# Projections: a quad's two first differences behind the weight split, and the fifth quad's sums in the second pair of units

## The chip, the core and the metric

The kernel runs on one core of a Trainium2 chip. TensorE (PE) multiplies, VectorE (DVE), ScalarE (ACT) and GpSimd (POOL) work elementwise, and SyncE (SP) issues most of the transfers. The metric is the device time of one launch in microseconds: the median of three runs, and beside it the span of one profiled execution, from its first to its last instruction.

## The reference

Two layers on a sequence of 256 rows, 2048 wide, with 32 heads of 128, all in float32. Cut to what matters here:

```
h = rms_norm(x, a_norm);  q, k, v, g = split(h @ a_w_in, 4)          # 2048 -> 4 x 4096
o = chunked attention with a relative-position bias
x = x + (o * silu(g)) @ a_w_out                                      # 4096 -> 2048
h_kv = rms_norm(x, kv_norm);  k, v = split(h_kv @ kv_w, 2)           # 2048 -> 2 x 4096
h = rms_norm(x, b_norm);  q, g = split(h @ b_w_in, 2)
o = forgetting attention (causal, decayed by cumulated log gates)
x = x + (o * silu(g)) @ b_w_out                                      # 4096 -> 2048
out = rms_norm(x, final_norm)
```

The change is in the two output projections, `@ a_w_out` (called ao) and `@ b_w_out` (called bo), each 256 x 4096 times 4096 x 2048.

## The kernel before

**Units and blocks.** The 2048 output columns of a projection are four units of 512 columns (ao0 to ao3). A unit sums over 16 blocks of 256 rows of the weight. A block is one transfer of 512 KB into a `raw` buffer (L207, issued by SP; six buffers, `RAW`). Float32 precision comes from splitting every operand in a rounded part and its rest: ACT copies raw to `hi` (L248), DVE subtracts `lo = raw - hi` (L249), and PE multiplies x.hi by w.hi, x.hi by w.lo and x.lo by w.hi (L185). There are four `hi` and four `lo` buffers (`SPLIT`), so the splits run four steps ahead of PE and then wait for PE to free a buffer. A plain block is 12 matmuls: two inner halves, two row tiles, three products.

**Quads.** For some blocks a 2 x 2 product of half blocks is made with seven products instead of eight (`class Quad`). A quad takes block b of two neighbouring units at once, `one` and `two` (two raw buffers), and is four steps for the feeder: i0 splits `one`, i1 splits two differences `t`, i2 splits half of `two`, i3 splits `one` again, after it was overwritten with two more differences. The first differences are `t0 = two0 - one0` (L289) and `t1 = two1 - two0` (L290); the later ones are L298 and L299, which overwrite `one`. Their ACT halves are L295, their DVE halves L296. On PE a quad is 21 matmuls (L528 to L530) and needs four combinations of the activations for its block, the *sums*: five small DVE operations (L380 to L386), an ACT copy (L387) and a DVE rest (L388), made by `Quads.sum_up` one quad after the other when the generator `ao_quads.open` is advanced.

**Order of the work.** `Quads.order` puts the quads between the plain blocks, three plain blocks from one quad to the next. The first pair of units (ao0, ao1) has 13 plain blocks, quad 0, three plain blocks, quad 1, three, quad 2, and the last seven; that is 29 steps. The second pair (ao2, ao3) has four plain blocks and five quads with three blocks between, then six. bo has quads only in its second pair, placed likewise. `project` walks these steps, and after each one lets side work advance by a list of step counts: for `ao_quads.open` the list was `[3, 1, 1, 2, 2]`, so the sums of quad blocks 0 to 4 are made after steps 3, 4, 5, 7 and 9. Block 4 is used by the second pair alone, since the first has three quads.

**What orders the engines.** Each engine works through its queue in order. The order in it is set when the program is built, by a scheduler which places an instruction as soon as what it depends on allows, by its own estimate. Two devices hold an instruction back. `feed.behind(dst, n)` (L265) makes ACT write one column of `dst` from a finished `hi` tile, so that whoever writes `dst` later stands behind that split; it was used for t0's half of `t`. `tc.issue_after(ins)` holds what is issued under it until behind the instruction `ins` in the order; `feed.by_dve` is the last L249 or L296 given out, `feed.by_act` the last L248 or L295. `t1` writes the other half of `t` and was held back by neither.

Of the kernel before, what the change touches and what calls it, by code (L numbers as in the profile page):

```python
# [2 lines left out]

# [49 lines left out]
QUADS = 5  # L53
# [13 lines left out]
def r32(ap):  # L67
    return ap.bitcast(F32)
# [8 lines left out]
def trunk(ctx, tc, x, x_t, gains, a_w_in, a_rel, a_w_out, kv_w, f_w, f_b, b_w_in, b_w_out, final_norm, out):  # L77
    nc = tc.nc
    pe, act, dve, pool, sp = nc.tensor, nc.scalar, nc.vector, nc.gpsimd, nc.sync
# [66 lines left out]
    def finish(side):  # L146
        advance(side, 99)
# [130 lines left out]
    class Quad:  # L278
# [4 lines left out]
        def split(self, i):  # L283

            one, two = self.raw
            t = self.all.t[:, 0]
            if not i:
                feed.behind(t[:, :, 0, :1], -1)
                dve.tensor_sub(t[:, :, 0], two[:, :, 0], one[:, :, 0])  # L289
                dve.tensor_sub(t[:, :, 1], two[:, :, 1], two[:, :, 0])  # L290
            src = [one, t, two[:, :, 1:], one][i]
            n = src.shape[2]
            hi = stream.tile([P, IL, KB, HN], F32R, name=f"quad_hi{i}", tag="hi", bufs=SPLIT)
            lo = stream.tile([P, IL, KB, HN], F32R, name=f"quad_lo{i}", tag="lo", bufs=SPLIT)
            feed.by_act = act.activation(hi[:, :, :n], src, AF.Copy)  # L295
            feed.by_dve = dve.tensor_sub(lo[:, :, :n], src, r32(hi[:, :, :n]))  # L296
            if not i:
                dve.tensor_sub(one[:, :, 0], two[:, :, 1], t[:, :, 0])  # L298
                dve.tensor_sub(one[:, :, 1], one[:, :, 1], one[:, :, 0])  # L299
            return hi, lo  # L300
# [89 lines left out]
    def spec(name, w, nk, late=0, kept=0, g0=None, quads=0):  # L390


        return dict(name=name, w=w, nk=nk, late=late, kept=kept, g0=g0, plain=nk // KB - quads)
# [8 lines left out]
    woven = [(qkvg[u], b) for u, b in WOVEN]  # L402
    todo = woven + [i for i in whole(qkvg[1]) if i not in woven]

    a_quads = Quads("a", None)
    a_pairs = [Quad(a_quads, qkvg[2 * g:2 * g + 2], KD // KB - 1, True, True) for g in range(1, NG)]
    for quad in a_pairs:
        first, second = (whole(sp_) for sp_ in quad.specs)
        todo += first[:QUAD_STEP] + [(None, quad)] + first[QUAD_STEP:] + second
    ao = [spec(f"ao{u}", a_w_out[u], KI) for u in range(4)]  # L410
    ao_quads, bo_quads = Quads("ao", a_w_out), Quads("bo", b_w_out)
    ao_order = ao_quads.order(ao[0], ao[1], 3, 13) + ao_quads.order(ao[2], ao[3], QUADS, 4)
    todo += ao_order
    for g in range(NG):
# [2 lines left out]
    bo = [spec(f"bo{u}", b_w_out[u], KI, LATE if u == 3 else 0, KEPT if u == 3 else 0) for u in range(4)]  # L417
# [6 lines left out]
    feed = Feed(todo)  # L424
# [36 lines left out]
    def project(lhs, specs, order, begun, closed, sides):  # L461


        units = {}

        def get(u):
            if u not in units:
                units[u] = Unit(lhs, specs[u])
            return units[u]

        for sp_, b in order:
            if sp_:
                us = [int(sp_["name"][-1])]
                get(us[0]).step(b)
            else:
                us = [int(u["name"][-1]) for u in b.specs]
                b.step(lhs, *(get(u) for u in us))
            for u in us:
                begun(u, units[u].left)
            for side, steps in sides:  # L480
                if steps:
                    steps[0] -= 1
                    while steps and steps[0] <= 0:
                        next(side, None)
                        steps.pop(0)
            for u in us:
                if not units[u].left:
                    more = closed(u, units[u].acc)
                    if more:
                        sides.append(more)  # L490
        for side, _ in sides:
            finish(side)
# [39 lines left out]
    def attention(g, biases, qk, vg, half, ocat, queues=(pool,) * NQ, line=(None, None), home=None):  # L532
# [50 lines left out]
        gT = z[:, :, HG * NB:].rearrange("p i (t h) u -> p h t i u", t=NT)  # L583
        yield
        ph, pl = split([pT[:, i, :NT] for i in range(HG)], "wide", line[1])
        yield
        op = bank("op").rearrange("p (i s) -> p i s", i=HG)
# [101 lines left out]
    oA = Stat("oA", KI)  # L689

    def side_a(g, accs):
        tb = att.tile([P, HG, S], F32, name="tb", tag="tb")
        for lo_, hi_, c0 in ((0, CHUNK, CHUNK), (CHUNK, P, 0)):
            sp.dma_start(out=tb[lo_:hi_, :, c0:], in_=bass.AP(
                tensor=a_rel.tensor, offset=a_rel.offset + g * HG * NREL + REL + 1 - P + lo_ + c0,
                ap=[[1, hi_ - lo_], [NREL, HG], [1, S - c0]]))

        def biases():
            pool.memset(tb[:CHUNK, :, :CHUNK], NEG)
            return tb[:, :, ::-1], tb[:, :, P - 1::-1]  # L700

        qk = rows(UN, "qk")
        if g:
            for t in range(NT):
                dve.scalar_tensor_tensor(qk[:, t], accs["qk"][t], rsA[:, t:t + 1], a_quads.comb[:, t],
                                         op0=OP.mult, op1=OP.add)
        else:
            evac_scaled(accs["qk"], 0, UN, rsA, qk)
        yield

        def vg():
            return accs["v"], accs["g"]

        yield from attention(g, biases, qk, vg, halfA, oA, (pool, pool, pool, act), (2, 2), home)
# [31 lines left out]
    rs, prev = [], None  # L746
    for g in range(NG):
# [15 lines left out]
        old, prev = prev, side_a(g, accs)  # L763
# [55 lines left out]
                           accum_out=ssq1[:, t, u:u + 1])  # L819
        return more and (more, [8, 7, 1, 1, 1] if u % 2 else [11, 1, 1, 1])  # L820

    project(oA, ao, ao_order, ao_begun, ao_closed, [(prev, [1, 0, 2, 6, 2, 1]), (ao_quads.open(oA, QUADS), [3, 1, 1, 2, 2])])
    tot1 = const.tile([P, NT], F32, name="tot1")
    dve.tensor_reduce(tot1, ssq1, axis=AX.X, op=OP.add)
    rsB, halfB = rstd_of(tot1, "b")
# [73 lines left out]
    def side_b(g, accs):  # L899
        cb = att.tile([P, HG, S], F32, name="cb", tag="tb")  # L900
        sp.dma_start(out=cb, in_=bass.AP(tensor=cumd.tensor, offset=cumd.offset + g * HG * S,
                                           ap=[[0, P], [S, HG], [1, S]]))

        def biases():
            d0 = att.tile([P, HG, P], F32, name="d0")
            for i in range(HG):
                h = g * HG + i
                act.activation(d0[:, i], cb[:, i, :P], AF.Identity, bias=cum[:, 0, h:h + 1], scale=-1.0)
                act.activation(cb[:, i], cb[:, i], AF.Identity, bias=cum[:, 1, h:h + 1], scale=-1.0)
            for ap in (cb[:, :, P:], d0):  # L910
                pool.affine_select(out=ap, in_=ap, compare_op=OP.is_ge, fill=NEG, base=0,
                                   pattern=[[0, HG], [-1, P]], channel_multiplier=1)
            return cb, d0

        qk, gs = accs["q"]
        kv = accs["kv"]
        evac_scaled(kv, 0, GC, rsB, qk[:, :, GC:])
        rest_of = attention(g, biases, qk, lambda: (v, gs), halfB, oB, line=(1, 2), home=home)
        next(rest_of)
        yield  # L920
        v = v_split(kv, GC, rsB)
        yield
        yield from rest_of
# [8 lines left out]
    for g in range(NG):  # L932
# [3 lines left out]
        old, prev = prev, side_b(g, accs)  # L936
# [101 lines left out]
```

## Time and profile before

| | before |
|---|---|
| median of 3 runs | 1744.66 us (1743.78 to 1745.17) |
| the profiled execution | 1746.91 us, of which the span is 1745.2 us |
| granted TensorE clock, mean over the span | 0.998 |
| busy share of the span: PE, DVE, ACT, POOL | 99%, 79%, 65%, 30% |
| matmuls of the ao projection in the span | 697 to 868 us |
| matmuls of the bo projection in the span | 1569 to 1736 us |

A row of the timeline gives start and duration in us, the engine, the line, the operation, the tiles (out<-in), and in brackets the idle time of the engine before it and what ended that. A row of a wait list gives the total in us, how often, and the longest.

### The profile page before, as it was taken

The numbers are of one execution on the slowest core, as the hardware profiler recorded it, in microseconds if no ns is written. First come the engines' busy times: TensorE is split into PE (matmuls) and PEld (weight loads), VectorE is DVE, ScalarE is ACT, GpSimd is POOL, SyncE is SP. The second block draws the span as 40 slices with busy tenths as digits, with TensorE's granted clock in tenths as the row PEclk, the third lists the DMA queues.
The fourth block names the chain that finished last, engine by engine and source line by source line (L and its number), as shares of the span: only waits on it lengthen the run. The fifth ranks groups of instructions, "written<-read, shape, count | busy, mean of one in ns | idle before, by whom it ended". The sixth has DMA issues, their size and how long they took to land.

```text
span 1745.2 us, 25902 instructions
## 1 busy us (share of the span) xinstructions
PE 1725.5 (99%) x8303; PEld 1513.7 (87%) x8303; DVE 1375.6 (79%) x2066; ACT 1140.9 (65%) x2164; POOL 517.0 (30%) x1071
## 2 busy tenths in 40 slices
PE   9999999999999999999999999999999999999997
PEld 7888888888888888888888888888888888888886
DVE  7888888888888888888966777777777777776877
ACT  6666666666666666655657777777777777765554
POOL 1332333333333333112104333333333333333000
PEclk9999999999999999999999999999999999999999
DMA  8777777767777777666767777777777777777654
GB/s 294 247 230 225 235 229 229 232 227 227 225 228 229 231 227 226 196 235 238 245 214 231 227 227 226 227 226 225 226 228 223 227 225 227 250 224 233 225 194 145
DMA packets 143657, 396.38 MB, mean 227 GB/s; under 512 B 31104, under 2 KB 38560, under 8 KB 143392
## 3 DMA queue, kind: packets, MB, share of 16 engines
q1 hardware_dynamic: 107472, 354.25, 63.3%
q0 software_dynamic: 32256, 37.29, 6.6%
q10 hardware_dynamic: 3792, 3.17, 0.6%
q8 instruction: 66, 1.08, 0.3%
q14 instruction: 71, 0.58, 0.1%
HBM read 351.05 MB, written 4.23 MB: 204 GB/s over the span
## 4 chain that ended last, share of the span: by engine, by line
PE 91%; DVE 4%; DMA 3%; ACT 1%; issue 1%; SPq 0%; ACTq 0%; DVEq 0%
PE bkv_acc L185 19%; PE bqg_acc L185 19%; PE aqk_acc L185 16%; PE avg_acc L185 16%; PE bo_acc L185 8%; PE ao_acc L185 3%; DMA ao_raw<-in_a_w_out 2%; DVE ao_lo L249 1%; PE p L530 1%; PE p L529 1%; PE p L528 1%; DVE quad_lo L296 1%; PE s0p L552 1%; PE op L592 1%; PE s1p L530 0%
## 5 line engine op out<-in xcount | busy, mean ns | idle before, releaser
L502 POOL DMA_DIRECT2D sums<-first x448 | 219.9, 498 | 324.6 <-DVE wide L521 147.6
L502 POOL DMA_DIRECT2D sgZ<-sgY x512 | 250.7, 497 | 177.2 <-DVE sgY L499 96.5
L244 DVE SCALAR_TENSOR_TENSOR bqg_lo<-bqg_raw,gain,bqg_hi 128x512 fp32r<-128x512 f32 x256 | 182.8, 750 | 87.4 <-ACT bqg_hi L243 87.4
L243 ACT ACTIVATE bqg_hi<-bqg_raw,gain 128x512 fp32r<-128x512 f32 x256 | 170.9, 714 | 109.1 <-PE bqg_acc L185 51.3
L244 DVE SCALAR_TENSOR_TENSOR bkv_lo<-bkv_raw,gain,bkv_hi 128x512 fp32r<-128x512 f32 x256 | 180.1, 748 | 40.7 <-ACT bkv_hi L243 39.2
L185 PE MATMUL bqg_acc<-bqg_hi,x1Th 128*128 128x512 f32 x512 | 191.4, 384 | 0.0
L185 PE MATMUL bkv_acc<-bkv_hi,x1Th 128*128 128x512 f32 x512 | 189.0, 379 | 0.0
L185 PE MATMUL bkv_acc<-bkv_lo,x1Th 128*128 128x512 f32 x512 | 188.8, 379 | 0.0
L185 PE MATMUL bqg_acc<-bqg_lo,x1Th 128*128 128x512 f32 x512 | 188.8, 379 | 0.0
L185 PE MATMUL bkv_acc<-bkv_hi,x1Tl 128*128 128x512 f32 x512 | 188.8, 379 | 0.0
L185 PE MATMUL bqg_acc<-bqg_hi,x1Tl 128*128 128x512 f32 x512 | 188.8, 379 | 0.0
L243 ACT ACTIVATE bkv_hi<-bkv_raw,gain 128x512 fp32r<-128x512 f32 x256 | 167.5, 712 | 25.9 <-PE bqg_acc L185 20.0
L185 PE MATMUL aqk_acc<-aqk_hi,xTh 128*128 128x512 f32 x452 | 167.6, 382 | 1.4 <-ACT aqk_hi L248 1.4
L185 PE MATMUL avg_acc<-avg_hi,xTh 128*128 128x512 f32 x452 | 167.5, 382 | 0.2 <-ACT avg_hi L248 0.2
L185 PE MATMUL aqk_acc<-aqk_lo,xTh 128*128 128x512 f32 x452 | 166.3, 379 | 1.0 <-DVE aqk_lo L249 1.0
L185 PE MATMUL aqk_acc<-aqk_hi,xTl 128*128 128x512 f32 x452 | 166.1, 379 | 0.0
L185 PE MATMUL avg_acc<-avg_hi,xTl 128*128 128x512 f32 x452 | 166.1, 379 | 0.0
L185 PE MATMUL avg_acc<-avg_lo,xTh 128*128 128x512 f32 x452 | 166.1, 379 | 0.0
L248 ACT ACTIVATE avg_hi<-avg_raw 128x1024 fp32r<-128x1024 f32 x112 | 116.1, 1050 | 75.9 <-PE avg_acc L185 50.3
L249 DVE TENSOR_TENSOR avg_lo<-avg_raw,avg_hi 128x1024 fp32r<-128x1024 f32 x112 | 136.4, 1219 | 31.4 <-ACT avg_hi L248 31.4
L249 DVE TENSOR_TENSOR aqk_lo<-aqk_raw,aqk_hi 128x1024 fp32r<-128x1024 f32 x110 | 134.0, 1222 | 25.4 <-ACT aqk_hi L248 20.3
L248 ACT ACTIVATE aqk_hi<-aqk_raw 128x1024 fp32r<-128x1024 f32 x110 | 115.6, 1051 | 41.7 <-PE avg_acc L185 28.1
(348 smaller groups left out, 3927.5 us busy)
## 6 DMA issues: line engine op xcount, KB each, us to landing
bqg_raw<-in_b_w_in SPq DMA_DIRECT2D x128, 512.0 KB, 4.3
bkv_raw<-in_kv_w SPq DMA_DIRECT2D x128, 512.0 KB, 4.1
avg_raw<-in_a_w_in SPq DMA_DIRECT2D x127, 512.0 KB, 4.7
aqk_raw<-in_a_w_in SPq DMA_DIRECT2D x125, 512.0 KB, 4.6
ao_raw<-in_a_w_out SPq DMA_DIRECT2D x64, 512.0 KB, 4.4
bo_raw<-in_b_w_out SPq DMA_DIRECT2D x64, 512.0 KB, 4.2
sgZ<-sgY POOLq DMA_DIRECT2D x512, 40.0 KB, 4.0
sums<-first POOLq DMA_DIRECT2D x448, 32.0 KB, 3.7
```

The lines of the kernel that those rows point to most:

```text
L185: pe.matmul(acc[t], x[:, t * P:(t + 1) * P], w, start=t not in begun, stop=last and i == 2)
L243: act.activation(hi[:, :, j], raw[:, :, j], AF.Copy, scale=gk)
L244: dve.scalar_tensor_tensor(lo[:, :, j], raw[:, :, j], gk, r32(hi[:, :, j]), op0=OP.mult, op1=OP.subtract)
L248: self.by_act = act.activation(hi[:, :, j], raw[:, :, j], AF.Copy)
L249: self.by_dve = dve.tensor_sub(lo[:, :, j], raw[:, :, j], r32(hi[:, :, j]))
L296: feed.by_dve = dve.tensor_sub(lo[:, :, :n], src, r32(hi[:, :, :n]))
L502: queues[j].dma_start(out=r32(z)[j * SQ:(j + 1) * SQ, i], in_=y[i * SQ:(i + 1) * SQ, j])
L528: pe.matmul(out_, a[0], b[0], start=start, stop=False)
L529: pe.matmul(out_, a[0], b[1], start=False, stop=False)
L530: pe.matmul(out_, a[1], b[0], start=False, stop=stop)
L552: pe.matmul(s0p[:, i], q0[:, i], qkT[:, HG + i, 0], start=True, stop=True)
L592: pe.matmul(op[:, i, 1::NT], v1[:, i * DH:(i + 1) * DH], pT[:, i, NT], start=False, stop=i == HG - 1)
```

## The change

Two edits.

1. In the quads of ao and bo the one-column ACT write in front of t0 goes. Both first differences stand under `tc.issue_after(feed.by_dve.ins)` instead: behind the DVE half of the last weight split that was given out before the quad. The quads of the first layer's input projection (`a_quads`) keep what they had; the flag `w`, which was a weight and unused, now tells the two apart.
2. The last step count of `ao_quads.open` is 26 instead of 2. The sums of block 4 are made after step 33, the fourth plain block of the second pair, and no longer after step 9 of the first.

```diff
             if not i:
-                feed.behind(t[:, :, 0, :1], -1)
-                dve.tensor_sub(t[:, :, 0], two[:, :, 0], one[:, :, 0])
-                dve.tensor_sub(t[:, :, 1], two[:, :, 1], two[:, :, 0])
+                if not self.all.w:
+                    feed.behind(t[:, :, 0, :1], -1)
+                with tc.issue_after(feed.by_dve.ins) if self.all.w else nullcontext():
+                    dve.tensor_sub(t[:, :, 0], two[:, :, 0], one[:, :, 0])
+                    dve.tensor_sub(t[:, :, 1], two[:, :, 1], two[:, :, 0])
...
-    a_quads = Quads("a", None)
+    a_quads = Quads("a", False)
...
-    ao_quads, bo_quads = Quads("ao", a_w_out), Quads("bo", b_w_out)
+    ao_quads, bo_quads = Quads("ao", True), Quads("bo", True)
...
-    project(oA, ao, ao_order, ao_begun, ao_closed, [(prev, [1, 0, 2, 6, 2, 1]), (ao_quads.open(oA, QUADS), [3, 1, 1, 2, 2])])
+    project(oA, ao, ao_order, ao_begun, ao_closed, [(prev, [1, 0, 2, 6, 2, 1]), (ao_quads.open(oA, QUADS), [3, 1, 1, 2, 26])])
```

From L290 on a line of the changed kernel has a number two higher: t0 is L291 there, t1 L292, the rest of a quad's split L298, the later differences L300 and L301; the sums are L382 to L390, the transposed x1 pieces L152 as before.

The built programs show what becomes of it. PE's and POOL's order is the same throughout. Three places on DVE, each before and then after. In the names, `ao1_lo4` is the rest of block 4 of unit ao1, `ao0_raw1` and `ao1_raw1` are `one` and `two` of quad 1, `ao_quad` is `t` (and the scratch of the sums), and `ao_sums4` holds the sums of block 4.

From the end of quad 0 to the start of quad 1 in the first pair, before:

```order
L296 TENSOR_TENSOR quad_lo3_7433<-ao0_raw0_7222,quad_hi3_7432 128x1024
L290 TENSOR_TENSOR ao_quad_7184<-ao1_raw1_7343 128x2x256
L249 TENSOR_TENSOR ao1_lo4_7445<-ao1_raw4_7266,ao1_hi4_7444 128x1024
L249 TENSOR_TENSOR ao1_lo5_7457<-ao1_raw5_7291,ao1_hi5_7456 128x1024
L249 TENSOR_TENSOR ao0_lo15_7466<-ao0_raw15_7309,ao0_hi15_7465 128x1024
L289 TENSOR_TENSOR ao_quad_7184<-ao1_raw1_7343,ao0_raw1_7341 128x2x256
L296 TENSOR_TENSOR quad_lo0_7483<-ao0_raw1_7341,quad_hi0_7482 128x1024
```

The same place on DVE, after:

```order
L298 TENSOR_TENSOR quad_lo3_7424<-ao0_raw0_7222,quad_hi3_7423 128x1024
L249 TENSOR_TENSOR ao1_lo4_7436<-ao1_raw4_7266,ao1_hi4_7435 128x1024
L249 TENSOR_TENSOR ao1_lo5_7448<-ao1_raw5_7291,ao1_hi5_7447 128x1024
L249 TENSOR_TENSOR ao0_lo15_7457<-ao0_raw15_7309,ao0_hi15_7456 128x1024
L291 TENSOR_TENSOR ao_quad_7184<-ao1_raw1_7335,ao0_raw1_7333 128x2x256
L292 TENSOR_TENSOR ao_quad_7184<-ao1_raw1_7335 128x2x256
L298 TENSOR_TENSOR quad_lo0_7473<-ao0_raw1_7333,quad_hi0_7472 128x1024
```

t1, which reads only `two`, stood ahead of the three plain rests and now stands behind them and behind t0. At the other quads of ao and bo it goes behind the plain rests and t0 in the same way; at the last quad of bo it stands behind `quad_lo3` of the quad before, and t0 ahead of that, as it was.

Ahead of quad 0 of the first pair on DVE, before (from the last plain rest on):

```order
L249 TENSOR_TENSOR ao1_lo3_7338<-ao1_raw3_7197,ao1_hi3_7337 128x1024
L383 TENSOR_TENSOR ao_quad_7184<-ao_quad_7184 128x128
L384 TENSOR_TENSOR ao_quad_7184<-ao_quad_7184 128x128
L385 TENSOR_TENSOR ao_quad_7184<-ao_quad_7184 128x128
L289 TENSOR_TENSOR ao_quad_7184<-ao1_raw0_7224,ao0_raw0_7222 128x2x256
L386 TENSOR_TENSOR ao_quad_7184<-ao_quad_7184 128x128
L296 TENSOR_TENSOR quad_lo0_7361<-ao0_raw0_7222,quad_hi0_7360 128x1024
L388 TENSOR_TENSOR ao_sums4_7329<-ao_quad_7184,ao_sums4_7329 128x512
L298 TENSOR_TENSOR ao0_raw0_7222<-ao1_raw0_7224,ao_quad_7184 128x2x256
```

The same place, after:

```order
L249 TENSOR_TENSOR ao1_lo3_7330<-ao1_raw3_7197,ao1_hi3_7329 128x1024
L390 TENSOR_TENSOR ao_sums2_7238<-ao_quad_7184,ao_sums2_7238 128x512
L291 TENSOR_TENSOR ao_quad_7184<-ao1_raw0_7224,ao0_raw0_7222 128x2x256
L292 TENSOR_TENSOR ao_quad_7184<-ao1_raw0_7224 128x2x256
L298 TENSOR_TENSOR quad_lo0_7352<-ao0_raw0_7222,quad_hi0_7351 128x1024
L300 TENSOR_TENSOR ao0_raw0_7222<-ao1_raw0_7224,ao_quad_7184 128x2x256
```

The sums of block 4 are gone from here; t1 of quad 0, which had stood three weight splits earlier, comes in behind t0.

The end of quad 0 of the second pair on DVE, before:

```order
L296 TENSOR_TENSOR quad_lo2_7907<-ao3_raw0_7752,quad_hi2_7906 128x2x256
L296 TENSOR_TENSOR quad_lo3_7933<-ao2_raw0_7750,quad_hi3_7932 128x1024
L290 TENSOR_TENSOR ao_quad_7184<-ao3_raw1_7855 128x2x256
L249 TENSOR_TENSOR ao2_lo9_7945<-ao2_raw9_7788,ao2_hi9_7944 128x1024
L249 TENSOR_TENSOR ao2_lo10_7957<-ao2_raw10_7807,ao2_hi10_7956 128x1024
```

The same place, after:

```order
L298 TENSOR_TENSOR quad_lo2_7895<-ao3_raw0_7741,quad_hi2_7894 128x2x256
L382 TENSOR_TENSOR ao_quad_7184<-oAh1_185,oAl1_189 128x512
L385 TENSOR_TENSOR ao_quad_7184<-ao_quad_7184 128x128
L386 TENSOR_TENSOR ao_quad_7184<-ao_quad_7184 128x128
L387 TENSOR_TENSOR ao_quad_7184<-ao_quad_7184 128x128
L388 TENSOR_TENSOR ao_quad_7184<-ao_quad_7184 128x128
L298 TENSOR_TENSOR quad_lo3_7929<-ao2_raw0_7739,quad_hi3_7928 128x1024
L390 TENSOR_TENSOR ao_sums4_7910<-ao_quad_7184,ao_sums4_7910 128x512
L249 TENSOR_TENSOR ao2_lo9_7941<-ao2_raw9_7777,ao2_hi9_7940 128x1024
L249 TENSOR_TENSOR ao2_lo10_7953<-ao2_raw10_7796,ao2_hi10_7952 128x1024
```

Here the sums of block 4 came in, six of them ahead of and around `quad_lo3`, and t1 of the next quad left. On ACT the sums' copy (L387, now L389) and two small copies of x1 pieces (L151) stand ahead of the three weight copies that follow. Thirteen one-column ACT writes (L265) are gone, eight in ao and five in bo. On SP the load of x for unit ao1 (L793) is issued two weight loads earlier, ahead of block 15 of ao0.

More of the change, by code (lines that the diff above doesn't have):

```diff
@@ L1 @@
 import numpy as np
-from contextlib import ExitStack
+from contextlib import ExitStack, nullcontext
 import concourse.bass as bass
```

## The prediction

> **What bounds the kernel now.** I read the page first: PE is busy for nearly the whole span, so only time in which PE waits can be won.
>
> ```profile
> span 1745.2 us, 25902 instructions
> PE 1725.5 (99%) x8303; PEld 1513.7 (87%) x8303; DVE 1375.6 (79%) x2066; ACT 1140.9 (65%) x2164; POOL 517.0 (30%) x1071
> ```
>
> Next the waits of PE (total us, times, longest). Behind the start of the kernel, these are all above 0.2 us:
>
> ```profile
> PE ao_acc L185 <- DVE ao_lo L249: 4.7, 3, 1.7
> PE bo_acc L529 <- DVE quad_lo L296: 1.2, 1, 1.2
> PE ao_acc L529 <- DVE quad_lo L296: 0.8, 1, 0.8
> PE ao_acc L528 <- ACT quad_hi L295: 0.3, 1, 0.3
> ```
>
> Then the timeline of PE, for their places: three in ao's first pair, one in its second, one in bo. The first row is the start of quad 0.
>
> ```profile
> 733.07 0.38 PE L528 MATMUL p<-quad_hi,oAh 128*128 128x512 f32 x1
> 737.13 0.48 PE L528 MATMUL ao_acc<-quad_hi,oAh 128*128 128x512 f32 x1 [0.31 <-ACT quad_hi L295]
> 738.39 0.48 PE L529 MATMUL ao_acc<-quad_lo,oAh 128*128 128x512 f32 x1 [0.78 <-DVE quad_lo L296]
> 741.33 0.48 PE L185 MATMUL ao_acc<-ao_lo,oAh 128*128 128x512 f32 x1 [1.38 <-DVE ao_lo L249]
> 755.58 0.48 PE L185 MATMUL ao_acc<-ao_lo,oAh 128*128 128x512 f32 x1 [1.68 <-DVE ao_lo L249]
> 827.41 0.48 PE L185 MATMUL ao_acc<-ao_lo,oAh 128*128 128x512 f32 x1 [1.63 <-DVE ao_lo L249]
> 1707.30 0.48 PE L529 MATMUL bo_acc<-quad_lo,oBh 128*128 128x512 f32 x1 [1.16 <-DVE quad_lo L296]
> ```
>
> A stall costs a little more than its bracket, since matmuls overlap. The chain of waits gives the rest: the spacing of undisturbed matmuls, and the first matmul of quad 2, of the second pair's quad 0, and of its quad 4.
>
> ```profile
> 763.40 0.22 PE p L528
> 767.93 28.49 PE ao_acc L185 x132
> 796.42 0.22 PE p L528
> 847.88 0.22 PE p L528
> ```
>
> The spacing is 28.49/132 = 0.2158 us. Quad 0 to quad 2 is two rounds of 21 + 36 = 57 matmuls, 24.60 us; it took 763.40 - 733.07 = 30.33, so **5.73 us** are lost. 763.40 to 796.42 is 153 matmuls, 33.02, nothing lost. 796.42 to 847.88 is four rounds, 49.21, and took 51.46: **2.25 us** lost.
>
> Why, is on DVE. Around quad 1:
>
> ```profile
> 750.28 1.23 DVE L296 TENSOR_TENSOR quad_lo<-ao_raw,quad_hi 128x1024 fp32r<-128x1024 f32 x1 [1.93 <-ACT quad_hi L295]
> 753.70 0.69 DVE L290 TENSOR_TENSOR ao_quad<-ao_raw 128x512 f32<-128x512 f32 x1 [2.19 <-DMA ao_raw<-in_a_w_out]
> 754.30 3.49 DVE L249 TENSOR_TENSOR ao_lo<-ao_raw,ao_hi 128x1024 fp32r<-128x1024 f32 x3
> 757.71 0.68 DVE L289 TENSOR_TENSOR ao_quad<-ao_raw,ao_raw 128x512 f32<-128x512 f32 x1
> 758.31 1.22 DVE L296 TENSOR_TENSOR quad_lo<-ao_raw,quad_hi 128x1024 fp32r<-128x1024 f32 x1
> 750.53 1.06 ACT L248 ACTIVATE ao_hi<-ao_raw 128x1024 fp32r<-128x1024 f32 x1 [0.29 <-PE ao_acc L530]
> 751.83 2.00 ACT L248 ACTIVATE ao_hi<-ao_raw 128x1024 fp32r<-128x1024 f32 x2 [0.24 <-PE p L530]
> 748.38 0.33 SPq L207 DMA_DIRECT2D ao_raw<-in_a_w_out  x1
> ```
>
> t1 (L290) waits 2.19 us for `two` of the next quad, whose load SP could issue only at 748.38. The plain rests (L249) stand behind it in DVE's queue, though the first one's `hi` was there at 751.59. PE wants that rest at 755.58 - 1.68 = 753.90 and gets it at 755.5.
>
> **The change part by part.** *t1 behind the rests, quad 1.* DVE is free at 751.5. The rests run from 751.6, the third when its `hi` is there (753.83), to about 755.0; the first is done at 752.8, 1.1 before PE wants it. Then t0 755.0, t1 755.6, first quad rest 756.2, where it was 758.31. A quad's front is 0.6 longer for t1, but starts 2.7 earlier. The stall goes whole.
>
> *Quad 0's end (741.33) and 827.41* have the same form. For the latter:
>
> ```profile
> 822.15 1.23 DVE L296 TENSOR_TENSOR quad_lo<-ao_raw,quad_hi 128x1024 fp32r<-128x1024 f32 x1 [1.73 <-ACT quad_hi L295]
> 825.53 0.69 DVE L290 TENSOR_TENSOR ao_quad<-ao_raw 128x512 f32<-128x512 f32 x1 [2.15 <-DMA ao_raw<-in_a_w_out]
> 822.41 1.06 ACT L248 ACTIVATE ao_hi<-ao_raw 128x1024 fp32r<-128x1024 f32 x1 [0.29 <-PE ao_acc L530]
> ```
>
> `hi` is there at 823.5, the rest would be done at 824.7, and PE wants it at 825.8. t0, now the first to wait for the load, comes behind three rests, at 827.0, and the load was there at 825.5. These take 1.5 us of margin; PE's loss of 2.25 in this pair goes.
>
> *Quad 0 itself (737.13, 738.39).* Here DVE was late as a whole:
>
> ```profile
> 720.91 0.69 DVE L290 TENSOR_TENSOR ao_quad<-ao_raw 128x512 f32<-128x512 f32 x1 [2.16 <-DMA ao_raw<-in_a_w_out]
> 726.80 0.69 DVE L380 TENSOR_TENSOR ao_quad<-oAh,oAl 128x512 f32<-128x512 f32 x1
> 723.78 0.73 ACT L520 ACTIVATE wide<-sgZ 128x256 fp32r<-128x256 f32 x2
> 737.11 1.23 DVE L296 TENSOR_TENSOR quad_lo<-ao_raw,quad_hi 128x1024 fp32r<-128x1024 f32 x1 [0.25 <-ACT quad_hi L295]
> ```
>
> The wait of 2.16 goes, and so do the fifth sums: L380 and L388 at 0.60 apart, four small ones at 0.20, 2.0 us. DVE could be up to 4.2 earlier. What comes next is the fourth `hi` buffer, which PE frees when quad 0 starts: at 733.1, so copy to 734.2, rest to 735.4. PE wants it 16 matmuls into the quad, 733.07 + 3.45 = 736.5. It is in time by 1.1. So all of 5.73 goes in the first pair.
>
> *The fifth sums in the second pair* fall in the round in which DVE has most to do:
>
> ```profile
> 797.55 1.23 DVE L296 TENSOR_TENSOR quad_lo<-ao_raw,quad_hi 128x1024 fp32r<-128x1024 f32 x1 [2.32 <-ACT quad_hi L295]
> 807.50 1.24 DVE L499 STREAM_TRANSPOSE xinY<-xin 128x1024 f32<-128x1024 f32 x1
> 808.77 1.71 DVE L152 TENSOR_TENSOR x1Tl<-xinZ,x1Th 128x128 fp32r<-128x128 f32 x8
> 810.40 1.22 DVE L296 TENSOR_TENSOR quad_lo<-ao_raw,quad_hi 128x1024 fp32r<-128x1024 f32 x1
> ```
>
> Times in this paragraph are the old ones; the place itself moves with PE. The first 1.4 us of the sums lie in the idle 2.32 before 797.55. Their last 0.6 (L388) takes the place that t1 had behind it, so the plain rests start as before. From there DVE works without a pause, now with t1 between t0 and the quad: the last rest of quad 1 goes from 810.40 to 811.0 and ends at 812.2. PE starts that quad at 796.42 + 12.30 = 808.72 and wants the rest at 808.72 + 3.45 = 812.17. Bounds: 0, or 1.4 if the idle time does not take the sums; I take **+0.1**. On ACT the sums' copy (about 0.55) and two x1 copies (0.4) come ahead of three weight copies, so the next plain rest ends at 800.7; PE wants it 22 matmuls after 796.42, at 801.2. No cost.
>
> *bo.* There the loads came in time, but for the last quad:
>
> ```profile
> 1700.21 1.22 DVE L249 TENSOR_TENSOR bo_keep<-bo_raw,bo_keep 128x1024 fp32r<-128x1024 f32 x1 [0.99 <-ACT bo_keep L248]
> 1705.43 0.69 DVE L290 TENSOR_TENSOR bo_quad<-bo_raw 128x512 f32<-128x512 f32 x1
> 1706.03 1.22 DVE L296 TENSOR_TENSOR quad_lo<-bo_raw,quad_hi 128x1024 fp32r<-128x1024 f32 x1
> ```
>
> t1 goes from ahead of the late rest to behind it, 0.6 earlier; but the kept block's rest, which waits for its load, now stands one difference earlier, and t1 pushes the next plain rest. Bounds 0 and -1.3 (the whole stall); I take **-0.3**, nearer to 0 since the work in the queue is the same.
>
> *The rest.* Thirteen one-column ACT writes go, on an engine 65% busy: 0, unless PE waited for `hi` there, where only the 0.31 did. x for ao1 is loaded two weight loads earlier, into a buffer that is free by then: 0; the blocks behind it are used rounds later, and a load lands in a few us.
>
> Sum: -5.73 - 2.25 + 0.1 - 0.3 = **-8.2 us**. The profiled execution (1746.91, its span 1745.2) would take 1738.7 with a span of 1737.0; it stands 2.25 above the median of the runs, so the median goes from 1744.66 to **1736.5**.
>
> **The rivals.** *DVE becomes the bound in the second pair's full round.* That is the 0.1 above, if the queue does not run as dense as the old rows. From 797.55 to the end of quad 1's last rest stand two L296, L388, three L249 and so on, some 14.6 us by their spacing against a round of 12.30; if no operation overlapped the end of the one before (1.22 for each 1.14, 0.69 for 0.60, 0.29 for 0.20) it would be about 1.8 more: 1738.3. Against it: 3.49 us for three L249 of 1.22 each. [...]
>
> *Quad 0 stays late,* because ACT's L520 there waits for a transfer and not for DVE: then 1.75 (the two stalls, with their start-up) stay, 1738.2. For it: L520 starts only at 723.78. Against: 1.1 us of margin at the end.
>
> *The gain is given back,* at the seam to layer B or in the loads, up to all of it: 1742 to 1744.7. Against it: no wait of PE shows there.
>
> *Slower: the ring of raw buffers closes.* All of DVE's quad work now stands behind one wait for `two`, whose load goes out when the third rest of the quad before frees its buffer. That loop is: landing, t0 and t1 (1.2), then L296, L298, L296, L299, L296 (1.25 + 0.6 + 1.14 + 0.6 + 0.6), 5.4 us and the landing.
>
> ```profile
> DMA to landing us min/median/max: 3.1/4.4/6.7
> ```
>
> It is shorter than PE's round of 12.30 while a load lands in 6.9 us. Beyond, each of the ten rounds between quads loses the excess: at 7.7 the gain is gone, from 8.1 the kernel is slower by over 0.2%, at 9 it takes 1757. The longest load of ao took 6.7.
>
> **How the numbers follow.** My forecast (1735.3 to 1737.5) has 0.72. DVE's full round has 0.11, quad 0 stays late 0.07: both still faster. Given back: 0.06. Slower: 0.04. A difference of 0.2%, 3.5 us, is about what a measurement of this kernel can tell from none, so faster (below 1741.2) is 0.90, same 0.06, slower 0.04. The range goes from all stalls gone, bo's too, and the spread of the runs (1744.66 - 9.3 - 0.7 = 1734.7) to 1740.5, a little above both partial cases.
>
> **What would show it.** Right: no wait of PE for L249 in ao; first product of quad 0 to that of quad 2 in 24.6 us; four rounds in 49.2 to 49.4; t1 (L292) without idle time before it; in bo a wait of 0.5 to 1.2 left. Wrong: a new wait of PE for the quad's rest (L298) in the second pair, t0 (L291) idle for a load by more than 2 us, or a gain in ao that the end of the span does not show.

## The result and the profile after

| | before | after |
|---|---|---|
| median of ten runs each | 1744.06 us (1743.33 to 1745.17) | 1739.45 us (1738.73 to 1742.07) |
| ratio of the times | | 0.9975, 95% interval 0.9965 to 0.9984 |
| profiled execution | 1746.91, span 1745.2 | 1738.73, span 1737.0 |

The kernel became faster, by 4.6 us in the medians (2.8 to 6.1 by the interval) and not by the 8.2 of the forecast. 1739.45 lies in the stated range (up to 1740.5), 2.95 above the predicted 1736.5 and outside the 1735.3 to 1737.5 that had most of the chance. The two profiled executions, taken alone, differ by 8.18, as the sum had it. That the sum met the one and missed the other is what had to be explained.

The page after, and all of PE's waits behind the start of the kernel:

```profile
span 1737.0 us, 25888 instructions
PE 1723.2 (99%) x8303; PEld 1513.8 (87%) x8303; DVE 1377.9 (79%) x2066; ACT 1139.4 (66%) x2151; POOL 517.0 (30%) x1071
```

```profile
PE bo_acc L531 <- DVE quad_lo L298: 0.5, 1, 0.5
PE ao_acc L531 <- DVE quad_lo L298: 0.4, 1, 0.4
PE bo_acc L185 <- DVE bo_lo L249: 0.2, 1, 0.2
```

No wait for L249 is left in ao. The timeline of PE gives the starts of quad 0 and quad 2 in the first pair, of quad 0 and quad 4 in the second, and the places of the waits:

```profile
732.34 0.38 PE L530 MATMUL p<-quad_hi,oAh 128*128 128x512 f32 x1
756.95 0.38 PE L530 MATMUL p<-quad_hi,oAh 128*128 128x512 f32 x1
789.97 0.38 PE L530 MATMUL p<-quad_hi,oAh 128*128 128x512 f32 x1
839.84 0.38 PE L530 MATMUL p<-quad_hi,oAh 128*128 128x512 f32 x1
...
806.28 0.48 PE L531 MATMUL ao_acc<-quad_lo,oAh 128*128 128x512 f32 x1 [0.40 <-DVE quad_lo L298]
1698.64 0.48 PE L531 MATMUL bo_acc<-quad_lo,oBh 128*128 128x512 f32 x1 [0.47 <-DVE quad_lo L298]
1700.38 0.48 PE L185 MATMUL bo_acc<-bo_lo,oBh 128*128 128x512 f32 x1 [0.17 <-DVE bo_lo L249]
```

The first pair's two rounds take 24.61, with nothing lost. The second pair's four take 49.87 where 49.21 would be undisturbed: 0.66 is lost at 806.28. DVE between quad 1 and quad 2 of the first pair, the place at which t1 waited 2.19 us before:

```profile
745.98 1.23 DVE L298 TENSOR_TENSOR quad_lo<-ao_raw,quad_hi 128x1024 fp32r<-128x1024 f32 x1 [1.84 <-ACT quad_hi L297]
747.28 3.66 DVE L249 TENSOR_TENSOR ao_lo<-ao_raw,ao_hi 128x1024 fp32r<-128x1024 f32 x3
750.85 0.68 DVE L291 TENSOR_TENSOR ao_quad<-ao_raw,ao_raw 128x512 f32<-128x512 f32 x1
751.45 0.69 DVE L292 TENSOR_TENSOR ao_quad<-ao_raw 128x512 f32<-128x512 f32 x1
752.05 1.22 DVE L298 TENSOR_TENSOR quad_lo<-ao_raw,quad_hi 128x1024 fp32r<-128x1024 f32 x1
```

The three rests follow the quad's last rest at once, t0 and t1 come behind them without idle time, and the next quad's first rest behind those. Between quad 0 and quad 1, where t1 waited 1.11 us, the order is the same, without idle time too.

### The profile page after: what moved, and what is told of

Read it like the earlier page. It is cut to its first block, busy times and chain, and to the rows that moved or that the text cites. A ratio compares the mean times of both kernels' runs of the same rounds, so it can differ in the third digit from the quotient of the medians.

```text
span 1737.0 us, 25888 instructions
## 1 busy us (share of the span) xinstructions
PE 1723.2 (99%) x8303; PEld 1513.8 (87%) x8303; DVE 1377.9 (79%) x2066; ACT 1139.4 (66%) x2151; POOL 517.0 (30%) x1071
## 4 chain that ended last, share of the span: by engine, by line
PE 97%; DVE 1%; DMA 1%; ACT 1%; SPq 0%; issue 0%; DVEq 0%; ACTq 0%
PE bkv_acc L185 19%; PE bqg_acc L185 19%; PE avg_acc L185 17%; PE aqk_acc L185 16%; PE bo_acc L185 8%; PE ao_acc L185 7%; PE p L532 1%; PE p L531 1%; PE p L530 1%; PE s0p L554 1%; PE op L594 1%; PE op L532 0%; PE s1p L532 0%; PE s1p L531 0%; PE op L531 0%; PE op L530 0%
## 5 line engine op out<-in xcount | busy, mean ns | idle before, releaser
L249 DVE TENSOR_TENSOR avg_lo<-avg_raw,avg_hi 128x1024 fp32r<-128x1024 f32 x112 | 136.8, 1222 | 31.0 <-ACT avg_hi L248 31.0
L249 DVE TENSOR_TENSOR aqk_lo<-aqk_raw,aqk_hi 128x1024 fp32r<-128x1024 f32 x110 | 134.1, 1223 | 24.8 <-ACT aqk_hi L248 17.0
```

Source lines behind the costliest of these rows:

```text
L249: self.by_dve = dve.tensor_sub(lo[:, :, j], raw[:, :, j], r32(hi[:, :, j]))
```

## The experiments

The theory: in the kernel before, t1 holds DVE until a load has landed, and the plain rests behind it come late by that much; the first edit ends this, and the second adds little. The rivals: the fifth sums in front of quad 0 were the loss, or the profile misled. The table holds what the profile of each run showed; the starts of the quads are read from the timeline of PE as above. Undisturbed, the first two columns would be 24.60 and 49.21; for the third the lowest value measured, 9.84, has to serve. The runs were made on several chips. Each ratio below is to the kernel before, run beside it, and its medians lie close together (1744.06, 1744.50, 1744.48).

| run | profiled execution | first pair, two rounds | second pair, four rounds | bo, fourth to fifth quad |
|---|---|---|---|---|
| before, first profile | 1746.91 | 30.17 | 51.46 | 11.14 |
| before, second | 1743.62 | 28.36 | 50.76 | 10.98 |
| before, third | 1744.15 | 29.34 | 50.69 | 11.18 |
| before, fourth | 1743.43 | 28.46 | 51.09 | 10.62 |
| sums alone | 1745.15 | 28.66 | 51.46 | 10.97 |
| t1 alone, first | 1744.12 | 28.69 | 49.29 | 11.51 |
| t1 alone, second | 1740.49 | 26.75 | 49.29 | 11.04 |
| first edit alone | 1741.01 | 25.74 | 49.29 | 11.56 |
| changed kernel, first | 1738.73 | 24.61 | 49.87 | 10.89 |
| changed kernel, second | 1739.24 | 24.61 | 49.86 | 10.84 |
| sums after step 27 | 1738.55 | 25.12 | 49.29 | 10.66 |
| the same, kept rests apart, first | 1738.75 | 25.45 | 49.29 | 9.90 |
| the same, second | 1739.79 | 25.60 | 49.29 | 9.84 |

**The first edit alone.** The changed kernel with the sums where they were:

```diff
-(ao_quads.open(oA, QUADS), [3, 1, 1, 2, 26])
+(ao_quads.open(oA, QUADS), [3, 1, 1, 2, 2])
```

> The first edit alone: both first differences behind the last rest, the fifth block's sums still after step 9. Theory: the first edit carries the gain, since it takes t1's wait for its load out of the way of the plain rests. PE's waits for L249 in ao (4.7 us in the profile of before) are gone; the 2.0 us of sums stand ahead of quad 0 again, where the changed kernel has 0.9 idle and about 0.5 of margin on DVE, so 0.6 comes back there, and 0.4 of the changed kernel's stall in the second pair goes: changed kernel +0.2, 1739.1 to 1740.2. Rival: the sums ahead of quad 0 were worth the 1.75 us of its stalls: changed kernel + 1.75 - 0.4, about 1740.8.

Measured: 1739.93 median of 9, beside 1744.50 for before; ratio 0.9973 (0.9963 to 0.9983), the gain of the whole change. In ao it left one wait, of quad 0, and the 0.4 in the second pair went. The median lies in the theory's range, but the interval (about 1738 to 1741.5) holds the rival's 1740.8 too. In the profile 1.13 is lost at quad 0, between the 0.6 of the theory and the 1.75 of the rival; what is said below of ACT's copy out of `sgZ` divides it.

```profile
PE bo_acc L531 <- DVE quad_lo L298: 1.1, 1, 1.1
PE ao_acc L531 <- DVE quad_lo L298: 0.8, 1, 0.8
```

**The second edit alone.** The kernel before with the last step count 26.

> The second edit alone: the fifth block's sums after step 33, t1 ahead of the plain rests as before. Theory: only quad 0's own stalls go (0.3 + 0.8 on the profile of before, where the 2.0 us of sums stood ahead of it), the waits of PE for L249 stay, and up to 0.5 is lost in the second pair's full round: 1743.0 to 1744.2. Rival: the sums are worth the whole loss at quad 0, 1.75 us, and make room for the rests too: about 1742.0 or below.

Measured: 1744.94 median of 11; ratio 1.0005 (0.9996 to 1.0014): no gain, so both the theory's figure and the rival's were too good. The timeline shows why: quad 0's wait for its rest fell from 0.78 to 0.45 and its 0.31 for `hi` went, but the plain rest behind it is ruled by t1, which waits for its load whenever DVE gets there.

```profile
737.13 0.48 PE L529 MATMUL ao_acc<-quad_lo,oAh 128*128 128x512 f32 x1 [0.45 <-DVE quad_lo L296]
738.99 0.69 DVE L290 TENSOR_TENSOR ao_quad<-ao_raw 128x512 f32<-128x512 f32 x1 [1.91 <-DMA ao_raw<-in_a_w_out]
740.87 0.48 PE L185 MATMUL ao_acc<-ao_lo,oAh 128*128 128x512 f32 x1 [2.18 <-DVE ao_lo L249]
```

t1 waited 1.91 instead of 1.11, and PE behind it 2.18 instead of 1.38. The time won ahead of quad 0 was handed to the load. And 0.51 was lost where the sums now stand: the first two rounds of the second pair took 12.57 and 12.54, where all four profiles of the kernel before have 12.30 twice. The theory had up to 0.5 there.

**t1 alone.** The kernel before, with only t1 moved (the scheduler also mixes the small sums in front of quad 0 a little differently):

```diff
+                with tc.issue_after(feed.by_dve.ins) if self.all.w is not None else nullcontext():
-                dve.tensor_sub(t[:, :, 1], two[:, :, 1], two[:, :, 0])
+                    dve.tensor_sub(t[:, :, 1], two[:, :, 1], two[:, :, 0])
```

> The kernel before with one thing changed: t1 stands behind the last rest given out; t0 keeps its one-column ACT write, and the fifth block's sums stay after step 9. Theory: t1's wait for its load in front of the plain rests was the whole loss, so this alone brings the gain: no wait of PE for L249 in ao, 1739.3 to 1740.6, with 0.5 to 0.9 of wait left at quad 0 from the sums. Rival: t0 has to be behind the rest too, or the ACT write costs: 1741.5 to 1743.

Measured: 1740.11 median of 11, before 1744.48; ratio 0.9977 (0.9968 to 0.9985). One instruction in another place brings the gain; that t0 left the ACT write as well adds nothing that these runs can tell. No wait for L249 is left in ao. The waits at quad 0 sum to 1.40 in the first profile and 1.34 in the second, more than the expected 0.5 to 0.9. The first profile held something else besides, which the last of these sections shows.

**The kernel before again, unchanged, three times.** The first two expectations:

> The kernel before once more, unchanged, to see whether its stalls vary from execution to execution. Theory: t1's waits are for loads whose landing varies, and the profiled execution of before had late ones; this execution ends at 1743.3 to 1745.2, and PE's waits for L249 in ao sum to 2 to 4 us instead of 4.7, the time following them at about 1.35 us for 1. Rival: the profile itself lengthens an execution: again 1746.5 or more with 4.7 of waits.

> The kernel before a third time, unchanged. Theory, from the first two profiles (L249 waits of PE in ao 4.7 us with 1746.91, and 2.6 us with 1743.62): what varies is the landing of a quad's second buffer, which decides how long t1 holds DVE; the typical loss in ao is 5 to 6 us instead of 7.8, so 1743.3 to 1745.2 with L249 waits of 2.5 to 3.8. Rival: a first profile of a program is longer by itself: then about 1743.6 with 2.6 again.

Measured: 1743.62, 1744.15, and 1743.43 in the last one. Their waits, one fence for each:

```profile
PE ao_acc L185 <- DVE ao_lo L249: 2.6, 3, 1.2
```

```profile
PE ao_acc L185 <- DVE ao_lo L249: 3.4, 3, 1.3
```

```profile
PE ao_acc L185 <- DVE ao_lo L249: 2.9, 3, 1.3
```

The first profile had 4.7. Both theories hold: the waits and the times of the second and the third profile lie in their ranges. Nor is a first profile always the longer one: those of the changed kernel and of the kept rests were the shorter of two. At quad 1 of the first pair, t1's idle time and PE's wait in the second and the third profile:

```profile
751.03 0.69 DVE L290 TENSOR_TENSOR ao_quad<-ao_raw 128x512 f32<-128x512 f32 x1 [0.95 <-DMA ao_raw<-in_a_w_out]
752.91 0.48 PE L185 MATMUL ao_acc<-ao_lo,oAh 128*128 128x512 f32 x1 [0.43 <-DVE ao_lo L249]
```

```profile
751.76 0.69 DVE L290 TENSOR_TENSOR ao_quad<-ao_raw 128x512 f32<-128x512 f32 x1 [1.63 <-DMA ao_raw<-in_a_w_out]
753.64 0.48 PE L185 MATMUL ao_acc<-ao_lo,oAh 128*128 128x512 f32 x1 [1.11 <-DVE ao_lo L249]
```

The difference is 0.52 in both, and 0.51 in the first profile (2.19 and 1.68) and the fourth (0.89 and 0.38). At the wait in the second pair it is 0.51 or 0.52 in all four too: 2.15 and 1.63, 1.43 and 0.92, 1.53 and 1.02, 1.84 and 1.32. So PE's wait there follows the landing of the quad's second buffer microsecond for microsecond, above some 0.5 of slack. The same load took 5.3, 4.1, 4.7 and 4.0 us from issue to landing in the four profiles.

> The kernel before a fourth time. Theory, from the first three profiles (losses in ao's quad rounds, over 4 x 12.30 us, of 7.82, 5.31 and 6.23 with times of 1746.91, 1743.62 and 1744.15): the time is 1738.4 + that loss within 0.7, and the loss lies between 5 and 7. Rival: the time varies elsewhere as much as there, and the two don't go together.

The loss in ao was 5.74 (28.46 + 51.09 - 73.81), inside 5 to 7; 1738.4 + 5.74 is 0.71 above the time, a little outside the 0.7. bo's fourth round was the shortest of the four there.

**The changed kernel again.**

> The changed kernel once more, unchanged. Theory: its profiled execution (1738.73, the fastest of ten) had hardly a stall, and a typical one holds some tenths more: 1738.7 to 1740, with one or two waits of PE of 0.2 to 1 us that its first profile has not, at a rest or a first difference behind a late load. Rival: the waits are the same as in the first profile, and the difference lies outside PE's waits, in the granted clock or around the span.

Measured: 1739.24, with the waits of the first profile (0.4 in ao, 0.4 and 0.2 in bo). The rival holds for ao and bo. The 0.5 of difference is in neither: ao's matmuls began 0.1 later, and the stretch between ao's end and bo's begin took 0.5 longer.

**The sums after step 27.** The last step count 20 in the changed kernel:

> The changed kernel with the last step count 20 instead of 26: the fifth block's sums after step 27, in the plain blocks of unit ao1, where DVE has idle time. Theory: the changed kernel's wait of 0.4 us for a quad's rest in the second pair is the 2.0 us of sums in the round in which DVE has most to do; it goes, and four rounds of the second pair take 49.2 instead of 49.87. By the median 0.65 less than the changed kernel, 1738.6 to 1739.2. Rival: that wait has another cause (the turn of x and its x1 pieces, which stay there) and stays at 0.4, with the time of the changed kernel.

Measured: 1739.10 median of 6; ratio to before 0.9969 (0.9957 to 0.9981). The second pair's rounds fell from 49.87 to 49.29 and the wait there is gone, as expected. Against the changed kernel the medians can't be told apart. The 0.58 came back as 0.51 at quad 0 in this execution, which the next run follows up.

**The kept rests apart.** A kept block is one of the last unit whose `hi` and `lo` have buffers of their own (`bo_keep`). The run with the sums after step 27, and in addition:

```diff
-                self.by_dve = dve.tensor_sub(lo[:, :, j], raw[:, :, j], r32(hi[:, :, j]))
+                rest = dve.tensor_sub(lo[:, :, j], raw[:, :, j], r32(hi[:, :, j]))
+                if not 0 <= h < spec["kept"]:
+                    self.by_dve = rest
```

> As the run before, and the kept blocks' rests of the last unit don't count as the last rest given out, so that bo's last quad has its first differences behind the last plain rest, and one kept rest moves behind the quad's start. Theory: bo's remaining waits (0.5 for a quad's rest, 0.2 for a plain rest, in all 0.97 of matmul spacing) come from one kept rest and t0 that stand ahead of them on DVE; they go, the distance from bo's fourth to its fifth quad falls from 10.9 to 9.9: 1.6 less than the changed kernel, 1737.4 to 1738.3. Rival: the wait is for the kept block's load, and another rest waits instead: no less than the run before.

Measured: 1738.75 median of 5; ratio to before 0.9967 (0.9955 to 0.9980). The distance in bo fell to 9.90 as expected; the median by 0.7 instead of 1.6, not to be told from the changed kernel. The profiled execution took as long as that of the changed kernel. In it 0.85 was lost at quad 0 of the first pair and 0.53 between ao's end and bo's begin, much as in the second profile of the changed kernel, while ao began 0.33 earlier. In bo itself 0.42 of the 0.99 came back, since a new wait stands inside the fifth quad, here and, longer, in the second profile:

```profile
1708.70 0.48 PE L533 MATMUL bo_acc<-quad_lo,oBh 128*128 128x512 f32 x1 [0.15 <-DVE quad_lo L300]
```

```profile
1709.79 0.48 PE L533 MATMUL bo_acc<-quad_lo,oBh 128*128 128x512 f32 x1 [0.45 <-DVE quad_lo L300]
```

So bo took 166.27 from its first matmul to its last, and 166.50 in the second profile, where the changed kernel had 166.84 and 166.78: the distance alone says too much. The second profile:

> The best kernel so far once more. In its first profile quad 0 of the first pair lost 0.85 (13.15 instead of 12.30), where the gate sgZ landed at 723.44 and the copies of ACT that wait for it stand ahead of a weight copy; in the changed kernel it landed at 722.62 and nothing was lost. Theory: the loss at quad 0 follows that landing, counted back from the quad's start: up to 9.7 us ahead costs nothing, 8.6 us ahead 0.85; bo's distance from the fourth to the fifth quad is 9.9 again; 1738.0 to 1739.0. Rival: another operation decides, and the loss is the same 0.85 whatever the landing.

Measured: 1739.79, 0.8 above the expected range, with 0.99 lost at quad 0 and about 1.1 ahead of the projection (ao's first matmul at 697.18, and at 696.11 in the first profile). The mechanism of quad 0 is the expected one. ACT's copy out of `sgZ` (line 520 before, 524 here) waits for transfers on POOL's queue, which turn the attention weights of the last heads together with their gate; the copy takes the weights. It and the start of quad 0, in the first and the second profile of this kernel:

```profile
723.55 0.42 ACT L524 ACTIVATE wide<-sgZ 128x256 fp32r<-128x256 f32 x1 [2.49 <-DMA sgZ<-sgY]
732.01 0.38 PE L532 MATMUL p<-quad_hi,oAh 128*128 128x512 f32 x1
```

```profile
724.76 0.42 ACT L524 ACTIVATE wide<-sgZ 128x256 fp32r<-128x256 f32 x1 [2.63 <-DMA sgZ<-sgY]
733.08 0.38 PE L532 MATMUL p<-quad_hi,oAh 128*128 128x512 f32 x1
```

It starts 8.46 and 8.32 ahead of the quad, with 0.85 and 0.99 lost; 8.81 ahead in the run before, with 0.51. Each time the sum is 9.31 or 9.32. In the two profiles of the changed kernel it starts 9.62 and 9.50 ahead, and nothing is lost:

```profile
722.72 0.42 ACT L522 ACTIVATE wide<-sgZ 128x256 fp32r<-128x256 f32 x1 [1.34 <-DMA sgZ<-sgY]
```

So a transfer on POOL's queue that landed late cost PE up to 0.99 us at quad 0, in programs whose engines have the same order there as the changed kernel. Where the fifth sums stand in front of quad 0, the sum is larger: 8.85 and 1.13 in the first edit alone, 7.83 and 2.15 in the second profile of t1 alone, 9.98 both times. By this the sums are worth 0.67 at quad 0 and not the 1.75 of the rival, and the rest of both losses is the landing. This is read from five executions; moving that copy was not tried.

**t1 alone, again.** What the first profile held:

> The run with t1 alone moved, once more. Its first profile (1744.12, the slowest of its eleven) had nine matmuls in a row at 0.426 us instead of 0.216 right behind quad 0's waits, from 740.6 to 743.6, with a granted clock of 0.52: 2 us lost beside the 2.0 of the waits. Theory: that half clock is a chance event that some executions have behind a cluster of waits; this one has none, first to second quad in 13.3 to 14.4 instead of 16.38, 1739.0 to 1741.5. Rival: the waits at quad 0 bring it each time: again 16.4 and about 1744, though the median of eleven runs is 1740.11.

Measured: 1740.49, first to second quad 14.44, and the granted clock behind the waits was 1.00. The slices of the first profile, and of the second counted from the same place in the quad (us, then busy time and count of PE, PEld, DVE, ACT and POOL, granted clock, DMA share, GB/s):

```profile
737.00:740.00 3.00, 1.78 (x6) 1.03 (x7) 2.65 (x4) 3.00 (x5) 0.00 (x0) 1.00 0.51 175
740.00:743.00 3.00, 3.00 (x9) 2.43 (x8) 3.00 (x4) 2.20 (x3) 0.00 (x0) 0.52 0.76 233
743.00:746.00 3.00, 3.00 (x14) 2.53 (x14) 2.79 (x4) 0.89 (x1) 0.00 (x0) 0.91 0.97 351
```

```profile
736.00:739.00 3.00, 1.91 (x8) 1.13 (x7) 2.75 (x4) 3.00 (x4) 0.00 (x0) 1.00 0.56 186
739.00:742.00 3.00, 3.00 (x16) 2.62 (x15) 3.00 (x5) 1.63 (x3) 0.00 (x0) 1.00 0.83 249
```

Nine matmuls in 3 us at a clock of 0.52, where the second profile has sixteen.

## Why the prediction was right and where it was wrong

**t1 behind the rests.** Right. It is the cause of the gain (t1 alone and the first edit alone reach it, the second alone does not), and all of the loss at quads 0 and 1 and at 827.41 went. One slip: 5.73 was counted from a start in the timeline to one in the chain, and the chain has these starts 0.16 later (763.40 there, 763.24 in the timeline). It was 5.57.

**The fifth sums in the second pair.** Forecast +0.1, bounds 0 and 1.4; it was 0.66, of which 0.58 go with the sums. DVE's work from the rest at 791.26 to the end of the last one at 806.23 took 14.97 instead of 14.6:

```profile
791.26 1.23 DVE L298 TENSOR_TENSOR quad_lo<-ao_raw,quad_hi 128x1024 fp32r<-128x1024 f32 x1 [0.67 <-ACT quad_hi L297]
792.40 0.69 DVE L390 TENSOR_TENSOR ao_sums<-ao_quad,ao_sums 128x512 fp32r<-128x512 f32 x1
793.13 3.50 DVE L249 TENSOR_TENSOR ao_lo<-ao_raw,ao_hi 128x1024 fp32r<-128x1024 f32 x3
...
800.18 0.69 DVE L300 TENSOR_TENSOR ao_raw<-ao_raw,ao_quad 128x512 f32<-128x512 f32 x1
800.90 0.69 DVE L301 TENSOR_TENSOR ao_raw<-ao_raw 128x512 f32<-128x512 f32 x1
...
805.01 1.22 DVE L298 TENSOR_TENSOR quad_lo<-ao_raw,quad_hi 128x1024 fp32r<-128x1024 f32 x1
```

Two steps took 0.73 and 0.72 instead of 0.60: L390 to L249, for which the rows show no reason, and L300 to L301, which reads what L300 just wrote. Where the rest of `t` stands between these two, at the start of quad 2 of the first pair, L300's step is 0.61 (753.31 to 753.92). PE would have started the matmul of that rest at 805.72 (an estimate: the quad before started at 789.97, then a round of 12.30 and 16 matmuls, 3.45); the rest ended at 806.23 and the matmul came at 806.28, 0.56 late, for 0.40 of which PE stood idle. The rival that DVE becomes the bound was right in place and small in size; the three L249 in 3.50 show again that an operation starts before the one ahead has had its whole 1.22.

**bo.** -0.3 can't be seen. The distance was 10.62 to 11.18 in the five executions with t1 in its old place, and 10.66 to 11.56 in the six with t1 behind the rest and the kept rests as they were. What stalled there was the kept block's rest and t0 ahead of the quad; with both behind its start it was 9.90 and 9.84, but a wait inside the fifth quad took back 0.4 and 0.7 of that.

**Quad 0 stays late.** This rival is right in part: the wait for the transfer in front of L520 (L522 in the changed kernel) costs 0.5 to 1.0 in three executions of kernels with the same order there, and nothing in the two profiles of the changed kernel itself.

**Given back, and the ring of raw buffers.** Neither came. From the first matmul of layer B's q to the first of bo it took 701.24 before and 701.15 after. Loads of ao took up to 7.6 us after, more than the 6.9 of the loop, with no t0 idle: the longest ones were not those of a quad's second buffer, which took 6.1 at most.

**The step that failed is the last one of the sum:** "it stands 2.25 above the median of the runs, so the median goes from 1744.66". All of the difference between the two executions was carried over to the median. But the stalls that the change removes were for the most part what put the profiled execution above the rest: it lost 7.8 us in ao's quad rounds, the three others 5.3, 6.2 and 5.7. That is 2.1 of the 3.2 us by which it was longer than their mean; 0.7 more lay ahead of ao. So -5.73 - 2.25 was about 2 too large for the median. The changed kernel keeps 0.66 in the second pair, and its sum was to have 0.1. That gives 5.7 - 0.7 = 5.0 against 4.6 measured; where the last 0.4 lies is open, and a late quad 0 in some of the timed runs could be it. Also, of the 8.18 by which the spans differ, 0.55 was ao's first matmul at 696.44 instead of 696.99, before any changed instruction; ao itself gave 7.33 (170.80 and 163.47 from its first matmul to layer B's). And the profiled execution of the changed kernel is the fastest of its ten. That the profiled pair met the sum to 0.1 was partly chance. That the median lies in the range was partly chance too: the range reached up to 1740.5 for stalls that would stay, and the median got so far up mainly because there was less to remove. Of the signs named, one of being wrong came too, the new wait for L298 in the second pair.

## What to carry to other kernels

An instruction that waits for a load belongs behind the work in its queue that is ready: one difference in another place brought a gain not to be told from the whole one (0.23% and 0.25%), while taking 2 us of other work off the same queue there brought none, since the wait for the load took it up and the work cost 0.5 where it went. A stall that ended with a transfer varied here from execution to execution (at quad 1 of the first pair PE waited 1.68, 0.43, 1.11 and 0.38 us in four profiles of the same kernel), so a profiled execution that stands above all timed runs (here 1746.91 against 1743.33 to 1745.17 of ten) most likely holds larger stalls than usual (7.8 us in ao's quad rounds, the three others 5.3, 6.2 and 5.7), and its stalls are an upper estimate for the median. What a removed stall is worth is best read from two or three profiles of the unchanged kernel.

## What the runs showed of the hardware

In one profile of thirteen (t1 alone, the first) the granted clock fell behind a cluster of waits: it was 0.52 in the 3 us from 740 on, and 1.00 in the 3 us before. From 740.15 to 743.56, 3.41 us, the matmuls stood 0.426 us apart instead of 0.216, eight of them, which cost 1.7 us beside the waits. The longest of these waits was 0.78 us, in front of 739.40. What brings such a stretch on was not shown: the second profile has the same 0.78 at the same place, in front of 737.95, and its clock stayed at 1.00. Whether timed runs have such a stretch is open, as they carry no trace. A hint is their mean granted clock: it is 0.997 in three of all runs, this one, the next slowest of t1 alone (1743.04) and the slowest of the sums alone (1748.44), and 0.998 or 0.999 in the others, the 1746.91 of the first profile among them.
